# The last layer norm of a decoder layer: the last sums in two narrow parts, the root by ScalarE and one Newton step, shift vectors added by TensorE for three of four column quarters

## The chip, the cores and the metric

The kernel runs on one core of one Trainium2 chip. The core has TensorE (PE in the profile; its weight loads are PEld), VectorE (DVE), ScalarE (ACT), GpSimd (POOL) and SyncE (SP). SP and ACT also issue DMAs; the queues' own rows read SPq and ACTq. The metric is the device time of one execution in microseconds (us); before the change the median of three runs is 2263.68 us.

## The reference, cut to what matters

One decoder layer on 256 tokens of width 2048, all in float32. The change touches its last two lines alone:

```
alpha = (2.0 * DEPTH) ** 0.25
...
ple = jax.nn.sigmoid(h @ w_ple_gate[i]) * (p[i] @ w_ple_proj[i])
h = layer_norm(alpha * h + ple, ln_g[i, 3], ln_b[i, 3])

def layer_norm(x, g, b):
    mu = jnp.mean(xf, axis=-1, keepdims=True)
    var = jnp.mean(jnp.square(xf - mu), axis=-1, keepdims=True)
    y = (xf - mu) * lax.rsqrt(var + LN_EPS)
    return y * g + b
```

`h @ w_ple_gate` is a 256 x 2048 by 2048 x 2048 product. `p @ w_ple_proj` is made early in the kernel, parked in DRAM and read back as `ppr`. Each token's mean and variance go over all 2048 columns, so no value of a token can be normalised before the last column of that token is there.

## The kernel before, in words

Every large product is split for precision: the operands are cut into a high and a low part of the type fp32r, and a product is three matmuls (low x high, high x high, high x low; `Sum.add`, lines L394 to L396) of 128 x 128 weights and 512 moving columns, added up in PSUM. The weights from DRAM arrive as "units" of 256 rows by 1024 columns: SP issues the load into `rw_pg` (L169), ACT casts it to the high part `hw_pg` (L173), DVE subtracts to get the low part `lw_pg` (L177). Raw, high and low parts take one SBUF slot each out of 23, and a new tile takes a slot whose last use is over. A planner in the program sets the order in which these jobs stand among the others: it keeps count of the slots in use, `weights(n)` limits them to n, and `spend`, `after` and `clock` are its estimates of when DVE and TensorE get where. Its result is a fixed order on each engine. Each engine runs its instructions in that order and waits by semaphores.

The end of the kernel is `embedding`. The 256 tokens are two halves t = 0 and t = 1 of 128 tokens, one token to a partition; the columns are two blocks b = 0 and b = 1 of 1024. The sum before the norm, `y[b][:, t]`, reads `f2y` in the trace. A column block needs eight units, `w_pg` 0 to 7. For block 1 the first three units are used for both token halves as they come (`block`). The other five, HELD_END of them, are held and used for t = 0 first, then for t = 1, in column quarters c of 512. PSUM sums of block 0 read `w_pg` in the trace, those of block 1 `pg`.

`finish` (L1325 to L1334) takes a finished sum: ACT makes the sigmoid `sg` (L1327), DVE multiplies it by `ppr` (L1331), adds it to ALPHA times y (L1332) and takes the sums for mean and variance, bn_stats, per 512 columns (L1334). When all four quarters of a token half are in, `ln_stats` makes mean and variance of them (`mv`, bn_aggr, L528) and the reciprocal root by a start value from the bits and two steps (eight small DVE instructions, L491 to L516). `last_norm` then runs per quarter: `ln_normal`, that is (y - mean) * g (L536) and times root plus b (L537), and the store of 128 x 512 values (256 KB) to `out_h` (L1341). `g` and `b` are loaded to all partitions by `ln_vectors` (L522).

`later(n, job)` and `run_side` put a job n places on into the stream of units.

Of the kernel before, what the change touches and what calls it, by code (L numbers as in the profile page):

```python
# [8 lines left out]
F32 = mybir.dt.float32  # L9
# [21 lines left out]
SLOTS = 23  # L31
FRONT = 4
HELD = 3
HELD_END = 5
MATMUL = 0.227


# [76 lines left out]
def layer(ctx: ExitStack, tc: tile.TileContext, io):  # L114
# [208 lines left out]
    def done(u):  # L323
        room["used"] -= u.keeps
        fill()
# [16 lines left out]
    def later(n, job):  # L342
        while len(side) < n:
            side.append(idle)
        side.insert(n, job)
# [74 lines left out]
    def block(name, b, units, lhs, forms, sums, fold, before=None, host=False):  # L420
        sevens = [p for kind, p in units if kind == "S"]
        aux = None
        for j, (kind, p) in enumerate(units):
            if before is not None:
                before(j)
            u = take(name, b, p)
            if kind == "P":
                for c in range(2):
                    for kk in range(2):
                        some_products(u, p, lhs, sums, (0, 1), (c,), (kk,))  # L430
                    if host and not c:
# [86 lines left out]
    def ln_vectors(i):  # L518
        out = []
        for name in ("ln_g", "ln_b"):  # L520
            v = slot([P, D], F32, f"{name}{i}")
            sync.dma_start(v, io[name][0, i : i + 1, :].broadcast_to([P, D]))  # L522
            out.append(v)
        return out
# [8 lines left out]
    def ln_normal(y, t, mv, rstd, g, b, k0, nk):  # L533
        x = y[k0 // 8][:, t, k0 % 8 * P : (k0 % 8 + nk) * P]
        at = slice(k0 * P, (k0 + nk) * P)
        dve.scalar_tensor_tensor(x, x, mv[:, 0:1], g[:, at], ALU.subtract, ALU.mult)  # L536
        dve.scalar_tensor_tensor(x, x, rstd, b[:, at], ALU.mult, ALU.add)  # L537
# [96 lines left out]
    def put_by(b, pt):  # L634
# [77 lines left out]
    def plain(n):  # L712
        return [("P", p) for p in range(n)]
# [225 lines left out]
    def flat(ps):  # L939
        return ps.rearrange("p a n -> p (a n)")  # L940
# [375 lines left out]
        return norm  # L1316


    def embedding(ht, norm, y):
        weights(12)  # L1320
        stats = small.tile([P, 2, 4, 6], F32, tag="stats", name="plst", bufs=1)
        lhs = lambda k: (ht[:, k, :S], ht[:, k, S:])
        e = [load_columns(pp, b, "ppr") for b in range(2)]

        def finish(b, ps, sg, t, at):  # L1325
            sl, s = y[b][:, t, at], sg[:, t, at]
            act.activation(s, ps, AF.Sigmoid)  # L1327
            after(clock["pe"] + 0.8)
            n = at.stop - at.start
            spend(n, n, n)  # L1330
            dve.tensor_tensor(s, s, e[b][:, t, at], ALU.mult)  # L1331
            dve.scalar_tensor_tensor(sl, sl, ALPHA, s, ALU.mult, ALU.add)  # L1332
            for c in range(at.start // 512, at.stop // 512):
                dve.bn_stats(stats[:, t, 2 * b + c, :], y[b][:, t, c * 512 : c * 512 + 512])  # L1334

        def last_norm(t, mv, rstd):
            out = io["out"][0, t * P : (t + 1) * P]
            for c in range(4):
                ln_normal(y, t, mv, rstd, g, b, 4 * c, 4)
                at = slice(c * 512, c * 512 + 512)  # L1340
                (act if t and c % 2 else sync).dma_start(out[:, at], y[c // 2][:, t, c % 2 * 512 : c % 2 * 512 + 512])  # L1341
# [5 lines left out]
        finish(0, flat(ps[0]), sg, 0, whole)  # L1347
        later(0, lambda ps=ps, sg=sg: finish(0, flat(ps[1]), sg, 1, whole))
# [201 lines left out]
```

## Time and profile before

| | us |
|---|---|
| three runs, median (lowest to highest) | 2263.68 (2263.54 to 2264.49) |
| the profiled execution, its own time | 2265.43 |
| its span, first to last instruction | 2263.6 |
| TensorE busy in it | 2243.4 (99%) |
| DVE busy | 2018.6 (89%) |
| ACT busy | 1212.8 (54%) |
| granted TensorE clock, mean | 0.998 |

A row of a timeline reads: start, duration, engine, line of the kernel, operation, output <- inputs, size, count; a bracket at its end gives the time that the engine had stood idle and who ended it. A row of groups has the count, the busy time and the mean duration in ns. Matmuls overlap: each row lasts about 0.39 us, but the next starts 0.227 us later.

### The profile page before, as it was taken

The numbers are of one execution on the slowest core, as the hardware profiler recorded it, in microseconds if no ns is written. First come the engines' busy times: TensorE is split into PE (matmuls) and PEld (weight loads), VectorE is DVE, ScalarE is ACT, GpSimd is POOL, SyncE is SP. The second block draws the span as 40 slices with busy tenths as digits, with TensorE's granted clock in tenths as the row PEclk, the third lists the DMA queues.
The fourth block names the chain that finished last, engine by engine and source line by source line (L and its number), as shares of the span: only waits on it lengthen the run. The fifth ranks groups of instructions, "written<-read, shape, count | busy, mean of one in ns | idle before, by whom it ended". The sixth has DMA issues, their size and how long they took to land.

```text
span 2263.6 us, 26904 instructions
## 1 busy us (share of the span) xinstructions
PE 2243.4 (99%) x10379; PEld 1862.3 (82%) x10379; DVE 2018.6 (89%) x1773; ACT 1212.8 (54%) x1025; POOL 0.7 (0%) x6
## 2 busy tenths in 40 slices
PE   9999999999999999999999999999999999999997
PEld 7888888888888888888887888888888888888886
DVE  7999999999998788899899978989899999889876
ACT  6555555555554454655555545455555555555541
POOL 0000000000000000000000000000000000000000
PEclk9999999999999999999999999999999999999999
DMA  9665665655677545355566655776566566565761
GB/s 315 202 217 175 214 206 185 192 200 206 218 264 272 184 142 199 129 196 192 169 214 213 192 215 196 270 230 208 179 201 217 190 204 216 177 216 211 285 255 54
DMA packets 246560, 465.34 MB, mean 206 GB/s; under 512 B 17696, under 2 KB 125728, under 8 KB 243872
## 3 DMA queue, kind: packets, MB, share of 16 engines
q1 hardware_dynamic: 245040, 462.05, 60.5%
q8 instruction: 81, 1.33, 0.2%
q10 hardware_dynamic: 1392, 1.57, 0.2%
q14 instruction: 47, 0.39, 0.0%
HBM read 455.17 MB, written 8.39 MB: 205 GB/s over the span
## 4 chain that ended last, share of the span: by engine, by line
PE 96%; DVE 2%; DMA 1%; issue 1%; SPq 0%; ACT 0%; ACTq 0%; DVEq 0%
PE f1g L396 5%; PE f1g L395 5%; PE f1g L394 5%; PE f2g L396 4%; PE f2g L395 4%; PE f2g L394 4%; PE rqk L355 3%; PE aqk L355 2%; PE f2d L396 1%; PE f1d L396 1%; PE f2d L394 1%; PE f1d L395 1%; PE f1d L394 1%; PE f2d L395 1%; PE rqk L363 1%; PE f1e L396 1%
## 5 line engine op out<-in xcount | busy, mean ns | idle before, releaser
L177 DVE TENSOR_TENSOR lf_gu<-rf_gu,hf_gu 128x2048 fp32r<-128x2048 f32 x94 | 211.4, 2286 | 3.5 <-ACT hf_gu L173 3.5
L173 ACT CAST hf_gu<-rf_gu 128x2048 fp32r<-128x2048 f32 x94 | 177.3, 1908 | 27.9 <-DMA rf_gu<-in_f_gu 16.0
L241 DVE TENSOR_TENSOR luf_gu<-uf_gu,huf_gu 128x2048 fp32r<-128x2048 f32 x79 | 180.5, 2285 | 2.6 <-ACT huf_gu L233 2.5
L221 ACT CAST hbf_gu<-rf_gu 128x1536 fp32r<-128x1536 f32 x79 | 115.7, 1483 | 82.8 <-DMA rf_gu<-in_f_gu 67.5
L228 ACT CAST huf_gu<-uf_gu 128x1024 fp32r<-128x1024 f32 x79 | 83.1, 1052 | 133.1 <-DVE uf_gu L227 129.7
L394 PE MATMUL f1g<-hf_gu,xt 128*128 128x512 f32 x384 | 149.6, 390 | 1.5 <-ACT hf_gu L132 1.5
L396 PE MATMUL f1g<-lf_gu,xt 128*128 128x512 f32 x384 | 149.9, 390 | 0.3 <-DVE lf_gu L133 0.3
L395 PE MATMUL f1g<-hf_gu,xt 128*128 128x512 f32 x384 | 149.4, 389 | 0.0
L177 DVE TENSOR_TENSOR lf_down<-rf_down,hf_down 128x2048 fp32r<-128x2048 f32 x60 | 136.2, 2288 | 14.7 <-ACT hf_down L173 6.8
L173 ACT CAST hf_down<-rf_down 128x2048 fp32r<-128x2048 f32 x60 | 114.1, 1913 | 49.4 <-DMA rf_down<-in_f_down 15.1
L237 DVE TENSOR_TENSOR lbf_gu<-rf_gu,hbf_gu 128x1536 fp32r<-128x1536 f32 x79 | 138.3, 1751 | 0.0
L396 PE MATMUL f2g<-lf_gu,ht 128*128 128x512 f32 x328 | 127.6, 389 | 0.0
L394 PE MATMUL f2g<-hf_gu,ht 128*128 128x512 f32 x328 | 127.6, 389 | 0.0
L395 PE MATMUL f2g<-hf_gu,ht 128*128 128x512 f32 x328 | 127.6, 389 | 0.0
L233 ACT CAST huf_gu<-uf_gu 128x1024 fp32r<-128x1024 f32 x79 | 83.2, 1053 | 30.1 <-DVE uf_gu L232 30.1
L227 DVE TENSOR_TENSOR uf_gu<-rf_gu 128x1024 f32<-128x1024 f32 x79 | 96.3, 1219 | 0.0
L394 PEld LDWEIGHTS f1g<-hf_gu,xt 128*128 128x128 f32 x384 | 72.1, 188 | 17.2 <-ACT hf_gu L132 2.5
L396 PEld LDWEIGHTS f1g<-lf_gu,xt 128*128 128x128 f32 x384 | 72.1, 188 | 17.0 <-DVE lf_gu L133 2.0
L395 PEld LDWEIGHTS f1g<-hf_gu,xt 128*128 128x128 f32 x384 | 72.1, 188 | 14.9
L395 PEld LDWEIGHTS f2g<-hf_gu,ht 128*128 128x128 f32 x328 | 61.6, 188 | 12.8
L394 PEld LDWEIGHTS f2g<-hf_gu,ht 128*128 128x128 f32 x328 | 61.6, 188 | 12.8
L396 PEld LDWEIGHTS f2g<-lf_gu,ht 128*128 128x128 f32 x328 | 61.6, 188 | 12.8
(1307 smaller groups left out, 6369.9 us busy)
## 6 DMA issues: line engine op xcount, KB each, us to landing
rf_gu<-in_f_gu SPq DMA_DIRECT2D x192, 512.0 KB, 5.5
rf_down<-in_f_down SPq DMA_DIRECT2D x176, 512.0 KB, 4.5
rf_gu<-in_f_gu SPq DMA_DIRECT2D x317, 256.0 KB, 4.4
rw_rv<-in_w_rv SPq DMA_DIRECT2D x32, 512.0 KB, 4.6
rw_mix<-in_w_mix SPq DMA_DIRECT2D x32, 512.0 KB, 4.6
rw_pg<-in_w_pg SPq DMA_DIRECT2D x32, 512.0 KB, 4.7
rgr<-in_w_in_f SPq DMA_DIRECT2D x24, 512.0 KB, 4.6
rga<-in_w_in_f SPq DMA_DIRECT2D x20, 512.0 KB, 5.1
```

The costliest lines, as they stand in the source:

```text
L173: act.copy(self.hi, self.raw)
L177: dve.tensor_tensor(self.lo, self.raw, self.hi, ALU.subtract)
L221: act.copy(self.hb, self.raw[:, 1:])
L227: dve.tensor_tensor(u[:, 0:2], raw[:, 1:3], raw[:, 0:1].broadcast_to([P, 2, 512]), ALU.add)
L228: act.copy(hu[:, 0:2], u[:, 0:2])
L233: act.copy(hu[:, 2:], u[:, 2:])
L237: dve.tensor_tensor(lb, raw[:, 1:], hb, ALU.subtract)
L241: dve.tensor_tensor(lu, u, hu, ALU.subtract)
L355: pe.matmul(ps[:, f], u.tile_of(kk)[0][:, f * P : (f + 1) * P], rhs(k), start=k == 0, stop=k == KD - 1,)
L394: pe.matmul(o, al, bh, start=first, stop=False)
L395: pe.matmul(o, ah, bh, start=False, stop=False)
L396: pe.matmul(o, ah, bl, start=False, stop=self.left == 0)
```

## The change

- HELD_END goes from 5 to 6: two units of block 1 are used for both token halves at once, six are held. `weights(14)` is set before the block.
- For t = 1 the last 512 columns are summed in two parts of 256 columns. `Parts` splits the moving operand: a product is then six matmuls of 256 columns in place of three of 512.
- The order of the held work is written out: t = 0 first quarter, one unit of t = 1 first quarter, t = 0 second quarter, the rest of t = 1 first quarter, then the two narrow parts. `finish` follows each piece. Four quarters of t = 0 are normalised before the last pieces of t = 1 are finished.
- For t = 1 bn_stats goes by 256 columns, eight groups instead of four.
- The statistics, an intermediate matrix and six small vectors live in one new slot tile, `ends`.
- For t = 1, y is multiplied by -g ahead of the mean (`turned_sign`) in three of the four quarters.
- The root of t = 1: ACT takes sqrt(4 var + 4 eps), DVE its reciprocal `half`, and one Newton step gives `minus`, the negative reciprocal root. ACT runs one sqrt on a constant first (`four_eps`, set by POOL at the start), which brings the load of its function table with it.
- For three quarters of t = 1 TensorE makes b + (minus * mean) * g in PSUM: an identity times b, ahead of time, plus a diagonal matrix `across` (128 x 128, by DVE) times g. These are six matmuls in float32, not fp32r. DVE then needs one instruction for a quarter: (-g y) * minus + PSUM. The last quarter goes the old way, on DVE, and comes first.
- The store of the last quarter comes first, on ACT; the other three follow on SP, ACT, SP.

On DVE, around the last three units of weights (`lw_pg`) of block 1. The numbers in a unit's name are its place and a tile number, `ends` and `plst` hold the statistics. Before:

```order
L177 TENSOR_TENSOR lw_pg_4_16119<-rw_pg_4_16083,hw_pg_4_16117 128x2048
L1331 TENSOR_TENSOR sg_15990<-sg_15990,ppr_15834 128x1024
L1332 SCALAR_TENSOR_TENSOR f2y_14613<-f2y_14613,sg_15990 128x1024
L1334 BN_STATS plst<-f2y_14613 128x6 x2
L177 TENSOR_TENSOR lw_pg_5_16163<-rw_pg_5_16114,hw_pg_5_16161 128x2048
L1331 TENSOR_TENSOR sg_15990<-sg_15990,ppr_15834 128x1024
L1332 SCALAR_TENSOR_TENSOR f2y_14613<-f2y_14613,sg_15990 128x1024
L1334 BN_STATS plst<-f2y_14613 128x6 x2
L177 TENSOR_TENSOR lw_pg_6_16199<-rw_pg_6_16158,hw_pg_6_16197 128x2048
L177 TENSOR_TENSOR lw_pg_7_16227<-rw_pg_7_16194,hw_pg_7_16225 128x2048
```

After:

```order
L177 TENSOR_TENSOR lw_pg_4_16121<-rw_pg_4_16085,hw_pg_4_16119 128x2048
L1347 TENSOR_TENSOR sg_15992<-sg_15992,ppr_15835 128x1024
L1348 SCALAR_TENSOR_TENSOR f2y_14615<-f2y_14615,sg_15992 128x1024
L1351 BN_STATS ends<-f2y_14615 128x6 x2
L177 TENSOR_TENSOR lw_pg_5_16176<-rw_pg_5_16116,hw_pg_5_16172 128x2048
L177 TENSOR_TENSOR lw_pg_6_16178<-rw_pg_6_16136,hw_pg_6_16174 128x2048
L1347 TENSOR_TENSOR sg_15992<-sg_15992,ppr_15835 128x1024
L1348 SCALAR_TENSOR_TENSOR f2y_14615<-f2y_14615,sg_15992 128x1024
L1351 BN_STATS ends<-f2y_14615 128x6 x4
L177 TENSOR_TENSOR lw_pg_7_16219<-rw_pg_7_16169,hw_pg_7_16217 128x2048
L1376 SCALAR_TENSOR_TENSOR f2y_14615<-f2y_14615,ln_g_16128 128x1024
```

Unit 6 moved ahead of the second `finish` of block 0, unit 7 stands alone behind it, and the first sign turn follows. In the slots, the high part of unit 7 now takes the place of the high part of unit 1 of the same block, and the low part of unit 5 that of the high part of unit 0; before, these two waited for block 0's units and earlier loads alone. The slot of `ln_b` was that of a raw unit that DVE frees and is now that of a unit that TensorE frees; unit 6's load stands behind it on SP.

On ACT, the end of the program. Before:

```order
L1327 ACTIVATE sg_16133<-pg_16130 128x1024
L1327 ACTIVATE sg_16133<-pg_16131 128x512
L1327 ACTIVATE sg_16133<-pg_16132 128x512
L1341 DMA out_h<-f2y_14613 128x512
L1341 DMA out_h<-f2y_15427 128x512
```

After:

```order
L1343 ACTIVATE sg_16135<-pg_16132 128x512 x2
L1343 ACTIVATE sg_16135<-pg_16133 128x512
L1343 ACTIVATE sg_16135<-pg_16134 128x256
L1343 ACTIVATE sg_16135<-pg_16133 128x256
L1426 ACT_TABLE_LOAD
L1426 ACTIVATE ends<-four_eps 128x1
L1431 ACTIVATE ends<-mv_16461,four_eps 128x1
L1363 DMA out_h<-f2y_15429 128x512
L1363 DMA out_h<-f2y_14615 128x512
```

Three sigmoids became five smaller ones, and the table load with its two roots stands between the last sigmoid and the stores.

On DVE, the end of the program (`f2y_14613` and `f2y_14615` are columns 0 to 1023, `f2y_15427` and `f2y_15429` columns 1024 to 2047). Before:

```order
L516 SCALAR_TENSOR_TENSOR rstd_16394<-nb,ncur 128x1
L536 SCALAR_TENSOR_TENSOR f2y_14613<-f2y_14613,mv_16392,ln_g_16126 128x512
L537 SCALAR_TENSOR_TENSOR f2y_14613<-f2y_14613,rstd_16394,ln_b_16128 128x512
L536 SCALAR_TENSOR_TENSOR f2y_14613<-f2y_14613,mv_16392,ln_g_16126 128x512
L537 SCALAR_TENSOR_TENSOR f2y_14613<-f2y_14613,rstd_16394,ln_b_16128 128x512
L536 SCALAR_TENSOR_TENSOR f2y_15427<-f2y_15427,mv_16392,ln_g_16126 128x512
L537 SCALAR_TENSOR_TENSOR f2y_15427<-f2y_15427,rstd_16394,ln_b_16128 128x512
L536 SCALAR_TENSOR_TENSOR f2y_15427<-f2y_15427,mv_16392,ln_g_16126 128x512
L537 SCALAR_TENSOR_TENSOR f2y_15427<-f2y_15427,rstd_16394,ln_b_16128 128x512
```

After:

```order
L1355 BN_AGGR mv_16461<-ends 128x2
L1432 TENSOR_SCALAR ends<-mv_16461 128x1
L1433 RECIPROCAL ends<-ends 128x1
L1434 TENSOR_SCALAR ends<-ends 128x1
L1435 SCALAR_TENSOR_TENSOR ends<-ends 128x1
L1436 TENSOR_SCALAR ends<-ident,ends,mv_16461 128x128
L1437 TENSOR_SCALAR ends<-ends 128x1
L536 SCALAR_TENSOR_TENSOR f2y_15429<-f2y_15429,mv_16461,ln_g_16128 128x512
L537 SCALAR_TENSOR_TENSOR f2y_15429<-f2y_15429,ends,ln_b_16130 128x512
L1444 SCALAR_TENSOR_TENSOR f2y_14615<-f2y_14615,ends,pls_16455 128x512
L1444 SCALAR_TENSOR_TENSOR f2y_14615<-f2y_14615,ends,pls_16456 128x512
L1444 SCALAR_TENSOR_TENSOR f2y_15429<-f2y_15429,ends,pls_16457 128x512
```

Eight instructions of 512 columns became five, three of which read what TensorE left in PSUM (`pls`).

The diff:

```diff
-HELD_END = 5
+HELD_END = 6
...
+    four_eps = const.tile([P, 1], F32, name="four_eps")
+    nc.gpsimd.memset(four_eps, 4.0 * LN_EPS)
...
+    class Parts:
+        def __init__(self, parts):
+            self.parts = parts
+
+        def add(self, left, right):
+            for j, part in enumerate(self.parts):
+                part.add(left, tuple(x[:, 256 * j : 256 * j + 256] for x in right))
...
-        stats = small.tile([P, 2, 4, 6], F32, tag="stats", name="plst", bufs=1)
+        ends = slot([P, 256], F32, "ends")
+        stats = [ends[:, at : at + 6 * n].rearrange("p (a b) -> p a b", b=6) for at, n in ((128, 4), (152, 8))]
+        across = ends[:, :P]
+        root, v4, half, square, minus, plus = (ends[:, at : at + 1] for at in range(200, 206))
...
-            for c in range(at.start // 512, at.stop // 512):
-                dve.bn_stats(stats[:, t, 2 * b + c, :], y[b][:, t, c * 512 : c * 512 + 512])
-
-        def last_norm(t, mv, rstd):
...
+            size = (512, 256)[t]
+            for c in range(at.start, at.stop, size):
+                dve.bn_stats(stats[t][:, (1024 * b + c) // size, :], y[b][:, t, c : c + size])
...
+        def turned_sign(c, n):
+            x = y[c // 2][:, 1, c % 2 * 512 : c % 2 * 512 + n]
+            spend(n)
+            dve.scalar_tensor_tensor(x, x, -1.0, g[:, 512 * c : 512 * c + n], ALU.mult, ALU.mult)
+
         later(0, lambda ps=ps, sg=sg: finish(0, flat(ps[1]), sg, 1, whole))
-        g, b = ln_vectors(3)
+        later(1, lambda: turned_sign(0, 1024))
...
-        sums = sums_of([[ps[0][:, 0], ps[0][:, 1]], [ps[1][:, 0], ps[2][:, 0]]], plain(PAIRS))
+        sums = sums_of([[ps[0][:, 0], ps[0][:, 1]], [ps[1][:, 0], None]], plain(PAIRS))
+        parts = [Sum(v[:, :256], 2 * PAIRS) for v in (ps[2][:, 0], ps[1][:, 1])]
+        sums[1][1] = Parts(parts)
         n = PAIRS - HELD_END
+        weights(14)
         block("w_pg", 1, plain(n), lhs, None, sums, None)
+        run_side(len(side))
...
-        for t in range(2):
-            for c in range(2):
-                for u, p in zip(us, held):
-                    some_products(u, p, lhs, sums, (t,), (c,))
-                    if t and c:
-                        done(u)
-                if t:
-                    finish(1, sums[t][c].ap, sg, t, slice(512 * c, 512 * c + 512))
-            if not t:
-                finish(1, flat(ps[0]), sg, 0, whole)
-            last_norm(t, *ln_stats(stats[:, t], 3, t, LN_EPS))
+        more(0, 0)
+        finish(1, sums[0][0].ap, sg, 0, slice(0, 512))
+        more(1, 0, slice(0, 1))
+        more(0, 1)
+        finish(1, sums[0][1].ap, sg, 0, slice(512, 1024))
+        mv = moments(0)
+        rstd = small.tile([P, 1], F32, tag="rstd", name="rstd30")
+        rsqrt(rstd, mv[:, 1:2], 1, LN_EPS)
+        more(1, 0, slice(1, HELD_END))
+        for c in range(3):
+            normal(c)
+        finish(1, sums[1][0].ap, sg, 1, slice(0, 512))
+        turned_sign(2, 512)
+        normal(3)
+        for j, part in enumerate(parts):
+            for u, p in zip(us, held):
+                for kk in range(2):
+                    hi, lo = u.piece(1, kk)
+                    at = slice(256 * j, 256 * j + 256)
+                    part.add(half_of(lhs(2 * p + kk), 1), (hi[:, at], lo[:, at]))
...
+            finish(1, part.ap, sg, 1, slice(512 + 256 * j, 768 + 256 * j))
+        act.activation(root, four_eps, AF.Sqrt)
+        shifts = [banks("pls0")[:, j] for j in range(2)] + [banks("pls1")[:, 0]]
+        for c in range(3):
+            pe.matmul(shifts[c], ident, b[:, 512 * c : 512 * c + 512], start=True, stop=False)
+        mv = moments(1)
+        act.activation(root, mv[:, 1:2], AF.Sqrt, bias=four_eps, scale=4.0)
+        dve.tensor_scalar(v4, mv[:, 1:2], 4.0, 4.0 * LN_EPS, ALU.mult, ALU.add)
+        dve.reciprocal(half, root)
+        dve.tensor_scalar(square, half, half, v4, ALU.mult, ALU.mult)
+        dve.scalar_tensor_tensor(minus, square, 3.0, half, ALU.subtract, ALU.mult)
+        dve.tensor_scalar(across, ident, minus, mv[:, 0:1], ALU.mult, ALU.mult)
+        dve.tensor_scalar(plus, minus, -1.0, None, ALU.mult)
+        for c in range(3):
+            pe.matmul(shifts[c], across, g[:, 512 * c : 512 * c + 512], start=False, stop=True)
+        ln_normal(y, 1, mv, plus, g, b, 12, 4)
+        store(1, 3, act)
+        for c in range(3):
+            x = columns(y, c)
+            dve.scalar_tensor_tensor(x, x, minus, shifts[c], ALU.mult, ALU.add)
+            store(1, c, (sync, act, sync)[c])
```

`more(t, c)` adds the held units' products for one token half and quarter, `normal(c)` is `ln_normal` and store for t = 0, `moments(t)` is the bn_aggr, and `store` takes the queue as an argument. `ln_vectors(3)` is called one statement earlier than before.

More of the change, by code (lines that the diff above doesn't have):

```diff
@@ L1332, in finish, with moments, columns, store @@
             dve.scalar_tensor_tensor(sl, sl, ALPHA, s, ALU.mult, ALU.add)
-            for c in range(at.start // 512, at.stop // 512):
-                dve.bn_stats(stats[:, t, 2 * b + c, :], y[b][:, t, c * 512 : c * 512 + 512])
-        def last_norm(t, mv, rstd):
[L1337 to L1341, printed above, removed]
+            size = (512, 256)[t]
+            for c in range(at.start, at.stop, size):
+                dve.bn_stats(stats[t][:, (1024 * b + c) // size, :], y[b][:, t, c : c + size])
+        def moments(t):
+            mv = small.tile([P, 2], F32, tag="mv", name=f"mv3{t}")
+            dve.bn_aggr(mv, stats[t].rearrange("p a b -> p (a b)"))
+            return mv
+        def columns(v, c):
+            return v[c // 2][:, 1, c % 2 * 512 : c % 2 * 512 + 512]
+        def store(t, c, queue):
+            at = slice(c * 512, c * 512 + 512)
+            queue.dma_start(io["out"][0, t * P : (t + 1) * P, at], y[c // 2][:, t, c % 2 * 512 : c % 2 * 512 + 512])
         ps, sums = norm.front("w_pg", 0, lhs, plain(PAIRS))
@@ L1354, in embedding, with normal @@
+        parts = [Sum(v[:, :256], 2 * PAIRS) for v in (ps[2][:, 0], ps[1][:, 1])]
+        sums[1][1] = Parts(parts)
         n = PAIRS - HELD_END
+        weights(14)
         block("w_pg", 1, plain(n), lhs, None, sums, None)
+        run_side(len(side))
         held = range(n, PAIRS)
         us = [take("w_pg", 1, p) for p in held]
-        for t in range(2):
-            for c in range(2):
-                for u, p in zip(us, held):
-                    some_products(u, p, lhs, sums, (t,), (c,))
-                    if t and c:
-                        done(u)
-                if t:
-                    finish(1, sums[t][c].ap, sg, t, slice(512 * c, 512 * c + 512))
-            if not t:
-                finish(1, flat(ps[0]), sg, 0, whole)
-            last_norm(t, *ln_stats(stats[:, t], 3, t, LN_EPS))
+        def normal(c):
+            ln_normal(y, 0, mv, rstd, g, b, 4 * c, 4)
+            store(0, c, sync)
@@ new lines, in more @@
+        def more(t, c, at=slice(0, HELD_END)):
+            for u, p in list(zip(us, held))[at]:
+                some_products(u, p, lhs, sums, (t,), (c,))
+        more(0, 0)
[7 more added lines that the diff above has]
+        more(1, 0, slice(1, HELD_END))
@@ new lines, in embedding @@
+        for c in range(3):
[9 more added lines that the diff above has]
+                    part.add(half_of(lhs(2 * p + kk), 1), (hi[:, at], lo[:, at]))
+                if j:
+                    done(u)
+            finish(1, part.ap, sg, 1, slice(512 + 256 * j, 768 + 256 * j))
```

1 line of the change is left out of this document (added).

## The prediction

> **What bounds the kernel now.** I read the page first: busy shares, then the chain that ended last.
>
> ```profile
> span 2263.6 us, 26904 instructions
> PE 2243.4 (99%) x10379; PEld 1862.3 (82%) x10379; DVE 2018.6 (89%) x1773; ACT 1212.8 (54%) x1025; POOL 0.7 (0%) x6
> PE 96%; DVE 2%; DMA 1%; issue 1%; SPq 0%; ACT 0%; ACTq 0%; DVEq 0%
> ```
>
> TensorE is busy for 99% of the span and is 96% of the chain. Nothing is gained before its last product, so the change must pay behind it. The timelines of the three engines from the start of column block 1 show that tail:
>
> ```profile
> 2205.51 0.39 PE L394 MATMUL pg<-hw_pg,ht 128*128 128x512 f32 x1
> 2248.81 0.39 PE L396 MATMUL pg<-lw_pg,ht 128*128 128x512 f32 x1
> ...
> 2235.63 1.03 ACT L1327 ACTIVATE sg<-pg 128x1024 f32<-128x1024 f32 x1 [22.56 <-PE pg L396]
> 2242.43 0.60 ACT L1327 ACTIVATE sg<-pg 128x512 f32<-128x512 f32 x1 [5.77 <-PE pg L396]
> 2249.23 0.60 ACT L1327 ACTIVATE sg<-pg 128x512 f32<-128x512 f32 x1 [6.20 <-PE pg L396]
> ...
> 2240.54 0.26 DVE L528 BATCH_NORM_AGGREGATE mv<-plst 128x2 f32<-128x24 f32 x1
> 2242.50 0.75 DVE L536 SCALAR_TENSOR_TENSOR f2y<-f2y,mv,ln_g 128x512 f32<-128x512 f32 x1
> 2248.30 0.68 DVE L1331 TENSOR_TENSOR sg<-sg,ppr 128x512 f32<-128x512 f32 x1
> 2250.35 0.68 DVE L1331 TENSOR_TENSOR sg<-sg,ppr 128x512 f32<-128x512 f32 x1
> 2252.51 0.26 DVE L528 BATCH_NORM_AGGREGATE mv<-plst 128x2 f32<-128x24 f32 x1
> 2254.46 0.75 DVE L536 SCALAR_TENSOR_TENSOR f2y<-f2y,mv,ln_g 128x512 f32<-128x512 f32 x1
> 2259.59 0.75 DVE L537 SCALAR_TENSOR_TENSOR f2y<-f2y,rstd,ln_b 128x512 f32<-128x512 f32 x1
> ```
>
> The block's 192 products start 43.30/191 = 0.2267 us apart; the last ends at 2249.20. The span ends 14.4 us later: 11.14 us of DVE (to 2260.34) and 3.26 us for the last store and the end of the program. DVE has no wait in these 11.14 us and comes late into them: at 2248.30 it begins on a quarter of t = 1 whose products were done before 2242.43, because the four normalisations of t = 0 (2242.50 to 2248.30, 1.45 a quarter) stand ahead. A quarter's `finish` takes 2.16 (2250.35 to 2252.51, so 0.72 a step), moments and root 1.95 (2252.51 to 2254.46), four quarters 5.88.
>
> **The change, part by part.** *Narrow products on TensorE.* 48 matmuls of 512 columns become 96 of 256. The nearest row is a group of such matmuls with 128 x 128 weights elsewhere; the next two rows are for the float32 products below:
>
> ```profile
> L363 PE MATMUL aqk<-ht,lf_(20, 0)_5329 x16: 277/283/283, 755.5 to 757.3; 128*128 128x256 f32 x16
> 1082.95 0.59 PE L1062 MATMUL rs<-rq,rk 128*128 128x256 f32 x2
> 1083.38 0.38 PE L1063 MATMUL rs<-rq,rk 128*128 128x128 f32 x2
> ```
>
> Sixteen in 1.8 us from first to last start: 0.12 each. So 96 x 0.12 - 48 x 0.2267 = +0.64 us. Bounds: 0.113 (half a wide one) makes it 0, 0.13 makes it +1.6. I take 0.12. The stream then ends at 2205.51 + 144 x 0.2267 + 96 x 0.12 = 2249.67; the last matmul, in flight 0.28, is out at 2249.83.
>
> *Weights, from the order.* Two units now take 11.04 us (each 18 wide, 12 narrow), so held work starts at 2216.55, and unit 7 is wanted five units of 6 x 0.2267 later, at 2223.35, its low part at 2223.8 (before: 2227.3 and 2227.7).
>
> ```profile
> 2196.73 0.33 SPq L522 DMA_DIRECT2D ln_b<-in_ln_b  x1
> 2200.04 6.24 SPq L169 DMA_DIRECT2D rw_pg<-in_w_pg  x4
> 2205.96 1.90 ACT L173 CAST hw_pg<-rw_pg 128x2048 fp32r<-128x2048 f32 x1
> 2206.09 1.23 DVE L1331 TENSOR_TENSOR sg<-sg,ppr 128x1024 f32<-128x1024 f32 x1 [7.20 <-ACT sg L1327]
> 2215.73 4.47 DVE L177 TENSOR_TENSOR lw_pg<-rw_pg,hw_pg 128x2048 fp32r<-128x2048 f32 x2
> ...
> 2210.00:2215.00 5.00, 5.00 (x23) 4.14 (x23) 4.93 (x4) 2.49 (x2) 0.00 (x0) 1.00 0.00 0
> ```
>
> Before, the last low part was ready at 2220.2. Now `ln_b` waits for TensorE's freeing of a slot, where unit 6's load waited (2200.04), and that load and unit 7's stand behind it on SP; ACT casts unit 6 at about 2208 and unit 7 only when TensorE has left unit 1, 2216.6 to 2218.5. On DVE unit 5 waits for TensorE to leave unit 0 (2211.2), then unit 6 to 2215.7, a `finish` of 1024 columns with four narrow bn_stats, 3.9 (twice 1.25, four times 0.36), then unit 7, 2219.6 to 2221.9. That is 1.9 us ahead of need: no stall. Cost nothing, but the cover has shrunk from 7.5 us to 1.9; beyond it each us late costs one.
>
> *DVE up to the last part.* t = 0 second quarter is out at 2234.4 (2216.55 + 36, 6 and 36 products), its sigmoid at 2235.03. From 2235.06 DVE has 2.16 + 1.95 + three normalisations 4.35 + `finish` of t = 1 first quarter 2.2 + sign turn 0.70 + fourth normalisation 1.45 + first narrow part 1.35 = 14.2, to 2249.2. The second narrow part's sigmoid is out at 2249.83 + 0.03 + 0.38 = 2250.24 (0.38 on the line through 1.03 and 0.60). DVE waits 1.0 us for it: what had made it late is gone, and TensorE and ACT are late next. The first sign turn (1.2 us) fits before 2225, where DVE waits for TensorE. POOL's memset of 128 x 1 joins six instructions that take 0.7 us in all, at the start, beside the first loads: nothing, at most 0.1.
>
> *Last part and mean.*
>
> ```profile
> L465 DVE TENSOR_TENSOR sums<-f2a 128x256 f32<-128x256 f32 x4 | 1.7, 422 | 0.0
> L1107 DVE SCALAR_TENSOR_TENSOR ret<-ro,gmv,eve 128x256 f32<-128x256 f32 x16 | 6.6, 476 | 0.0
> L1091 DVE BATCH_NORM_STATS2 gst<-ro 128x6 f32<-128x256 f32 x16 | 6.5, 407 | 3.6 <-PE ro L1086 3.6
> L1092 DVE BATCH_NORM_AGGREGATE gmv<-gst 128x2 f32<-128x6 f32 x16 | 2.9, 182 | 0.6
> L503 DVE TENSOR_SCALAR nb<-ncur,nv 128x1 f32<-128x1 f32 x8 | 2.2, 273 | 0.3
> L1011 DVE RECIPROCAL asm<-asm 128x4 f32<-128x4 f32 x8 | 1.4, 178 | 0.3
> L1015 DVE TENSOR_SCALAR asc<-asc,asm 128x128 f32<-128x128 f32 x16 | 3.9, 284 | 0.3
> ```
>
> Three steps of 0.42, 0.45 and 0.41 with gaps: 1.35, to 2251.6. bn_aggr took 0.18 on 6 numbers and 0.26 on 24, so 0.37 on 48: variance at 2252.0.
>
> *Root.* The table load has to be over by then. Rows of two earlier loads:
>
> ```profile
> 2.77 1.28 ACT L1420 ACT_TABLE_LOAD   x1 [2.77 <-issue]
> 4.06 0.20 ACT L1420 ACTIVATE warm<-warm 128x1 f32<-128x1 f32 x1
> 797.00 0.58 ACT L883 COPY ra<-aqk 128x512 f32<-128x512 f32 x1 [6.92 <-PE aqk L355]
> 797.61 1.28 ACT L995 ACT_TABLE_LOAD   x1
> ```
>
> The load starts 0.03 after the work ahead of it and the next instruction 0.01 behind it: 2250.27 to 2251.55, constant root to 2251.75. Hidden under 1.7 us of DVE, by 0.25. Then root 0.2 to 0.3 with the hop to ACT, reciprocal 0.2, square 0.3, `minus` 0.2, `across` 0.34 (the 0.28 above has one vector operand, not two): 2253.35. From bn_aggr's end to the first normalising step that is 1.4, against 1.69 before; the root itself saves little.
>
> *Normalising.* DVE: last quarter from 2253.4, 0.78 + 0.67, then three steps 0.67 apart, the third at 2256.18. TensorE: a float32 product of 256 columns took 0.43 (1082.95 to 1083.38, two records), so 0.86 for 512; three of them and 0.17 in flight from 2253.4 end at 2256.15. Both sides meet, so a cheaper product would give nothing. The b products run in TensorE's idle time, 2249.7 to 2252.3. Last DVE step 0.72: 2256.9.
>
> *Stores.*
>
> ```profile
> L1341 ACTq DMA_DIRECT2D out_h<-f2y x2: 351/356/362, 2257.5 to 2260.4; - x2
> DMA to landing us min/median/max: 2.2/2.3/2.3
> ```
>
> They come 0.7 apart, not 1.45. Bounds 0 and +0.7; I take +0.1, since two queues share them.
>
> *Sum.* The tail behind TensorE's last product was 11.14 + 3.26 = 14.4 and will be 7.07 + 3.36 = 10.43; TensorE ends 0.63 later: -3.3 us, span 2260.3. The profiled execution took 2265.43, 1.8 more than its span, and stands 1.75 above the median of the runs; the difference is carried to the median: 2263.68 - 3.3 = 2260.4, 0.15% faster. A measurement of this kernel can tell about 0.2% (4.5 us) from no change, so this counts as within.
>
> **Rivals.** *TensorE waits for unit 7* (slower). The place and the 1.9 us are above. Lost gain from 5.2 us late, slower by 0.2% from 9.7 us. For it: three loads of 1 MB now leave SP within about a us of 2200, and two casts wait for TensorE itself. Against: issued at 2200 to 2206 they had landed by 2210 (the window from 2210 to 2215 moved nothing, its last figure), and unit 7's cast waits until 2216.6 anyway. Time 2268 and more; 9%, of it 8% beyond 0.2%.
>
> [...]
>
> *TensorE's clock has halved when `across` comes.* The windows behind the last product:
>
> ```profile
> 2253.00:2254.00 1.00, 0.00 (x0) 0.00 (x0) 0.85 (x5) 0.00 (x0) 0.00 (x0) 1.00 0.00 0
> 2254.00:2255.00 1.00, 0.00 (x0) 0.00 (x0) 0.93 (x4) 0.00 (x0) 0.00 (x0) 0.62 0.00 0
> ```
>
> The granted clock (third from the end) fell about 5.0 us after TensorE stopped. Here it stands idle for 1.1 us between b and `across`. At half speed three products would take 2.6 us more: 2263.0; 4%. [...]
>
> *All small terms at their low ends* (faster by over 0.2%): narrow products at 0.113 (-0.6), DVE's narrow steps, bn_aggr and `across` 0.3 less, the hop to ACT 0.1, stores 0.1, and 0.4 from elsewhere in the run: 2258.9; 17%. Against: TensorE's 0.12 is measured.
>
> **Chances.** Forecast 65%, small terms low 17%, stall 9%, drain 5%, clock 4%. Faster 0.17; same 0.65 + 0.05 + 0.04 + 0.01 = 0.75; slower 0.08. The range reaches from the low ends, 2258.9, past the half clock, to 2263.2, and leaves out the stall and part of the low case.
>
> **What would show it.** Right: last narrow product ends near 2249.8, without a gap of TensorE at unit 7; DVE idles about 1 us before the second narrow part; the constant root ends before bn_aggr; the three last DVE steps run nearly without waits; the last one ends near 2256.9. Wrong: TensorE idle near 2223; the root waiting behind the table load; DVE waiting for `pls` by more than 0.3 a step; a last store landing more than 2.6 us after its issue.

## The result, and the profile after

The changed kernel takes 2261.85 us, the median of 22 runs (2259.84 to 2264.34); the kernel before, run beside it, 2264.85 us (22 runs, 2263.50 to 2267.64). The ratio is 0.9987 with a 95% interval from 0.9981 to 0.9993: 3.0 us between the medians, 0.13%, faster. The interval lies below 1, and the gain is smaller than the 0.2% that the prediction set as its bound. The kernel before itself came out 1.17 us higher than in the three runs that the prediction started from (2263.68).

Two profiles cannot simply be subtracted. The profiled execution after took 2264.34 us, the longest of the 22 runs, with a span of 2262.6, only 1.0 us less than before, although its tail is 2.8 us shorter. So I measure from S, the start of the first product of column block 1. In the changed kernel's timeline of TensorE that is 2207.35; before it was 2205.51.

```profile
2207.13 0.39 PE L396 MATMUL w_pg<-lw_pg,ht 128*128 128x512 f32 x1
2207.35 0.39 PE L394 MATMUL pg<-hw_pg,ht 128*128 128x512 f32 x1
```

| from S, us | before | predicted | after |
|---|---|---|---|
| TensorE's last `pg` product ends | 43.69 | 44.32 | 44.37 |
| variance of t = 1 ready | 47.26 | 46.49 | 46.57 |
| `across` ready | - | 47.84 | 48.12 |
| TensorE's third `across` product ends | - | 50.64 | 51.02 |
| DVE's last instruction ends | 54.83 | 51.39 | 51.80 |
| span ends | 58.09 | 54.79 | 55.25 |

The tail is 2.84 us shorter, which agrees with the runs' 3.0. The first lines of the page after:

```profile
span 2262.6 us, 27044 instructions
PE 2251.5 (100%) x10439; PEld 1870.4 (83%) x10439; DVE 2019.0 (89%) x1778; ACT 1215.7 (54%) x1030; POOL 0.7 (0%) x7
```

DVE's timeline, from the low part of unit 7 to the last step:

```profile
2221.26 2.27 DVE L177 TENSOR_TENSOR lw_pg<-rw_pg,hw_pg 128x2048 fp32r<-128x2048 f32 x1
...
2250.64 0.43 DVE L1351 BATCH_NORM_STATS2 ends<-f2y 128x6 f32<-128x256 f32 x1
2252.17 0.42 DVE L1347 TENSOR_TENSOR sg<-sg,ppr 128x256 f32<-128x256 f32 x1 [1.10 <-ACT sg L1343]
...
2253.55 0.37 DVE L1355 BATCH_NORM_AGGREGATE mv<-ends 128x2 f32<-128x48 f32 x1
...
2254.35 0.16 DVE L1433 RECIPROCAL ends<-ends 128x1 f32<-128x1 f32 x1 [0.23 <-ACT ends L1431]
...
2255.12 0.35 DVE L1436 TENSOR_SCALAR ends<-ident,ends,mv 128x128 f32<-128x128 f32 x1
...
2256.89 2.26 DVE L1444 SCALAR_TENSOR_TENSOR f2y<-f2y,ends,pls 128x512 f32<-128x512 f32 x3
```

TensorE's timeline behind its last `pg` product:

```profile
2251.56 2.74 PE L1429 MATMUL pls<-ln_b,ident 128*128 128x512 f32 x6
2255.53 2.84 PE L1439 MATMUL pls<-ln_g,ends 128*128 128x512 f32 x6 [1.23 <-DVE ends L1436]
```

ACT's timeline from the last sigmoid to the root:

```profile
2251.76 0.38 ACT L1343 ACTIVATE sg<-pg 128x256 f32<-128x256 f32 x1 [3.94 <-PE pg L396]
2252.16 1.28 ACT L1426 ACT_TABLE_LOAD   x1
2253.45 0.20 ACT L1426 ACTIVATE ends<-four_eps 128x1 f32<-128x1 f32 x1
2254.02 0.29 ACT L1431 ACTIVATE ends<-mv,four_eps 128x1 f32<-128x1 f32 x1 [0.36 <-DVE mv L1355]
```

DVE's first bracket is the new wait of 1.10 us for the second narrow part: DVE is no longer late, TensorE and ACT are. The constant root ends at 2253.65, 0.27 us before the variance (2253.92), so the table load is hidden. TensorE waits 1.23 us for `across`, and its three products are done at 2258.37. The chain of work that ended last passes over these products, where before it was DVE alone:

```profile
2255.12 0.36 DVE ends L1436
2255.48 0.04 issue
2255.53 2.86 PE pls L1439 x6
2258.38 0.02 issue
2258.41 0.75 DVE f2y L1444
```

### The profile page after: what moved, and what is told of

The parts are those of the page before. It is cut to its first block, busy times and chain, and to the rows that moved or that the text cites. A ratio compares the mean times of both kernels' runs of the same rounds, so it can differ in the third digit from the quotient of the medians.

```text
span 2262.6 us, 27044 instructions
## 1 busy us (share of the span) xinstructions
PE 2251.5 (100%) x10439; PEld 1870.4 (83%) x10439; DVE 2019.0 (89%) x1778; ACT 1215.7 (54%) x1030; POOL 0.7 (0%) x7
## 4 chain that ended last, share of the span: by engine, by line
PE 98%; DVE 0%; DMA 0%; issue 0%; ACT 0%; SPq 0%; ACTq 0%; DVEq 0%
PE f1g L394 5%; PE f1g L396 5%; PE f1g L395 5%; PE f2g L395 4%; PE f2g L396 4%; PE f2g L394 4%; PE rqk L355 3%; PE aqk L355 2%; PE f2d L396 1%; PE f1d L396 1%; PE f1d L394 1%; PE f2d L394 1%; PE f2d L395 1%; PE f1d L395 1%; PE rqk L363 1%; PE f2e L396 1%
```

## The experiments

DVE's end is read from S in each profile. In the one repetition it agreed within 0.01 us, while the time of the changed kernel's 22 runs spreads over 4.5 us. All figures of the table are in us, the first and the last two from S.

| run | `across` ready | TensorE's `across` products | DVE ends | span ends |
|---|---|---|---|---|
| before | - | - | 54.83 | 58.09 |
| after | 48.12 | 2.84 | 51.80 | 55.25 |
| after_again | 48.12 | 2.84 | 51.80 | 55.22 |
| order_only | - | - | 54.36 | 57.63 |
| all_on_dve | - | - | 53.64 | 57.02 |
| dve_root | 48.98 | 4.54 | 54.37 | 57.68 |
| wide_last | 48.51 | 4.54 | 53.89 | 57.24 |
| wide_warm | 48.51 | 2.84 | 52.19 | 55.53 |
| late_b | 48.12 | six products | 56.99 | 60.35 |
| no_constant_root | 49.40 | 4.43 | 54.66 | 58.03 |
| late_unit | 51.17 | 2.84 | 54.85 | 58.23 |
| three_engines | 48.12 | 0.96 (fp32r) | 50.94 | 55.16 |
| three_engines_384 | 50.00 | 0.97 (fp32r) | 52.82 | 57.04 |

### The order of work alone (order_only)

```diff
-        for j, part in enumerate(parts):
...
-            finish(1, part.ap, sg, 1, slice(512 + 256 * j, 768 + 256 * j))
-        act.activation(root, four_eps, AF.Sqrt)
...
+        for u, p in zip(us, held):
+            some_products(u, p, lhs, sums, (1,), (1,))
+            done(u)
+        finish(1, sums[1][1].ap, sg, 1, slice(512, 1024))
+        rsqrt(rstd, mv[:, 1:2], 1, LN_EPS)
+        for c in range(4):
+            ln_normal(y, 1, mv, rstd, g, b, 4 * c, 4)
+            store(1, c, (sync, act)[c % 2])
```

> Keeps the changed order of the held work (HELD_END 6, weights(14), t = 1 begun early, four normalisations of t = 0 ahead of the last pieces) and takes back all the rest: one last part of 512 columns, DVE's eight-step root, no sign turns, all four quarters of t = 1 on DVE. Measured from S, the first product of block 1, to DVE's last end: before 54.83 us, after 51.80. Theory (the order alone only takes DVE's lateness out of the front of the tail; the three quarters handed to TensorE carry most of the gain): last wide sigmoid out at S + 44.3, finish 2.16, moments and root 1.95, four quarters 5.88, so S + 54.3 to 54.5, 0.4 us better than before. Rival (DVE's lateness was the brake and the order carries the gain): near S + 52. In the device time the theory gives -0.4 us (0.02%), the rival -2.8 us (0.12%).

DVE ended at S + 54.36, as the theory said; the ratio to before is 0.9997 (0.9987 to 1.0006). Taking the lateness out of DVE's queue gave 0.47 us. In this run's timeline DVE even waits 2.89 us for the last sigmoid:

```profile
2251.32 0.69 DVE L1347 TENSOR_TENSOR sg<-sg,ppr 128x512 f32<-128x512 f32 x1 [2.89 <-ACT sg L1343]
2252.05 0.69 DVE L1348 SCALAR_TENSOR_TENSOR f2y<-f2y,sg 128x512 f32<-128x512 f32 x1
```

So the lateness that I read from the profile before had been a symptom: with it gone, the last sigmoid sets the same chain of finish, root and four quarters 0.47 us earlier, and no more.

### Three quarters handed back to DVE (all_on_dve)

```diff
-        for c in range(3):
-            pe.matmul(shifts[c], ident, b[:, 512 * c : 512 * c + 512], start=True, stop=False)
...
-        ln_normal(y, 1, mv, plus, g, b, 12, 4)
-        store(1, 3, act)
-        for c in range(3):
-            x = columns(y, c)
-            dve.scalar_tensor_tensor(x, x, minus, shifts[c], ALU.mult, ALU.add)
+        for c in range(4):
+            ln_normal(y, 1, mv, plus, g, b, 4 * c, 4)
...
```

> The changed kernel with TensorE's shift vectors and the sign turns taken out: all four quarters of t = 1 normalised on DVE, two steps each; ScalarE's root and the two narrow parts stay. Theory: DVE's stretch from the root on is four quarters of 1.45 us behind an end of the root at about S + 47.8, so its last end at S + 53.65, 1.85 us later than in the changed kernel (51.80). Rival (DVE waits for TensorE's float32 products by 1.2 us in the changed kernel, so handing the work back costs next to nothing): S + 51.8 to 52.2.

S + 53.64 against 53.65 expected: handing three quarters to TensorE is worth 1.84 us. The sum of the parts follows from the two runs: order 0.47 (54.83 to 54.36), narrow parts and ScalarE's root together 0.72 (to 53.64), TensorE's products 1.84 (to 51.80); together 3.03. These are the worths in this order of steps: no run has the later steps without the new order of work, so what they would bring with DVE late is not shown.

### DVE's root in the changed kernel (dve_root)

```diff
-        act.activation(root, four_eps, AF.Sqrt)
...
-        act.activation(root, mv[:, 1:2], AF.Sqrt, bias=four_eps, scale=4.0)
...
-        dve.scalar_tensor_tensor(minus, square, 3.0, half, ALU.subtract, ALU.mult)
+        rsqrt(plus, mv[:, 1:2], 1, LN_EPS)
+        dve.tensor_scalar(minus, plus, -1.0, None, ALU.mult)
```

> The changed kernel with DVE's eight-step reciprocal root for t = 1 in place of ScalarE's root and the Newton step, and one more small instruction for the sign; no table load at the end. Theory (a small DVE instruction costs 0.2 to 0.25 us with its gap; ScalarE's way saves what five of them cost, less two hops): `across` 0.65 us later, DVE's last end at S + 52.45. Rival (two hops between the engines eat it, the table load delays it): S + 51.8 or earlier.

DVE ended at S + 54.37, 2.57 us later than after: four times my 0.65. `across` was 0.86 late, in the theory's direction. The other 1.7 us are in the products, in this run's timeline of TensorE:

```profile
2254.06 4.54 PE L1434 MATMUL pls<-ln_g,ends 128*128 128x512 f32 x6 [2.10 <-DVE ends L1432]
```

DVE's timeline shows the steps that waited for them:

```profile
2257.11 0.75 DVE L1439 SCALAR_TENSOR_TENSOR f2y<-f2y,ends,pls 128x512 f32<-128x512 f32 x1 [0.96 <-PE pls L1434]
2258.64 0.75 DVE L1439 SCALAR_TENSOR_TENSOR f2y<-f2y,ends,pls 128x512 f32<-128x512 f32 x1 [0.78 <-PE pls L1434]
```

The same six matmul records took 4.54 us instead of 2.84, and DVE waited twice. The windows of the same run give the reason; the granted clock is the third figure from the end:

```profile
2254.02:2254.52 0.50, 0.46 (x1) 0.30 (x2) 0.50 (x1) 0.00 (x0) 0.00 (x0) 1.00 0.00 0
2254.52:2255.02 0.50, 0.50 (x2) 0.19 (x1) 0.47 (x2) 0.00 (x0) 0.00 (x0) 0.86 0.00 0
2255.02:2255.52 0.50, 0.50 (x2) 0.34 (x1) 0.50 (x2) 0.00 (x0) 0.00 (x0) 0.50 0.00 0
...
2258.02:2258.52 0.50, 0.50 (x1) 0.00 (x0) 0.00 (x0) 0.00 (x0) 0.00 (x0) 0.73 0.00 0
```

TensorE's clock fell to half in the midst of the products, after 2.10 us of idleness, and came back 3.4 us later.

### One wide last part (wide_last)

```diff
-        for j, part in enumerate(parts):
-            for u, p in zip(us, held):
...
-            finish(1, part.ap, sg, 1, slice(512 + 256 * j, 768 + 256 * j))
+        for u, p in zip(us, held):
+            some_products(u, p, lhs, sums, (1,), (1,))
+            done(u)
+        finish(1, sums[1][1].ap, sg, 1, slice(512, 1024))
```

> The changed kernel with one last part of 512 columns for t = 1 in place of two of 256; bn_stats stays at 256 columns. Theory: TensorE ends 0.64 us earlier (S + 43.7), but the sigmoid takes 0.60 instead of 0.38 and DVE's three steps on 512 columns 2.2 instead of 1.37, so the variance and with it DVE's last end comes 0.4 us later, S + 52.2. Rival (the second narrow part costs TensorE 0.64 us and brings nothing, since DVE is late anyway): 0.2 us or more earlier, S + 51.6.

`across` came 0.39 later, as expected, but DVE ended 2.09 later, at S + 53.89. TensorE was done 0.69 us earlier and `across` came later, so it stood idle for 2.31 us, and the products took 4.54 us once more. Both expectations had missed this.

### The wide part, with TensorE kept busy (wide_warm)

```diff
+        spare = banks("pls2")[:, 0]
+        for c in range(2):
+            pe.matmul(spare, ident, b[:, 512 * c : 512 * c + 512], start=True, stop=True)
```

> The wide last part of the run above it, with two more float32 products of identity and b into a PSUM tile that nobody reads, behind the three b products: TensorE then stands idle for about 0.6 us instead of 2.3 before `across` comes. Nothing of the computation is left out. With the wide part alone the three `across` products took 4.54 us (2.84 in the changed kernel) and DVE's last end came at S + 53.89. Theory (the 2.3 us of idleness let the granted clock fall to 0.50, and that was the whole difference): clock 1.00 throughout, three products 2.84 again, DVE's last end at S + 52.2, which is the 0.4 us later than the changed kernel that the wide part itself costs. Rival (TensorE is slowed by DVE's and ACT's traffic at that moment, or by the wide part's place): products stay above 4 us, S + 53.9.

Two products that nobody reads bring DVE's end 1.70 us forward against the kernel without them. TensorE's timeline without them (wide_last):

```profile
2248.38 2.73 PE L1422 MATMUL pls<-ln_b,ident 128*128 128x512 f32 x6
2253.42 4.54 PE L1432 MATMUL pls<-ln_g,ends 128*128 128x512 f32 x6 [2.31 <-DVE ends L1429]
```

And with them (wide_warm):

```profile
2248.89 2.74 PE L1422 MATMUL pls<-ln_b,ident 128*128 128x512 f32 x6
2251.47 1.88 PE L1425 MATMUL pls<-ln_b,ident 128*128 128x512 f32 x4
2253.93 2.84 PE L1435 MATMUL pls<-ln_g,ends 128*128 128x512 f32 x6 [0.59 <-DVE ends L1432]
```

The granted clock stayed at 1.00 until 2260, past DVE's end, and the end came at S + 52.19. So the wide part itself costs 0.39 us, and the fall of the clock 1.70. In the changed kernel the gap is 1.23 us, and the clock stayed at 1.00 through all its products.

### The b products on the path (late_b)

```diff
-        for c in range(3):
-            pe.matmul(shifts[c], ident, b[:, 512 * c : 512 * c + 512], start=True, stop=False)
...
-            pe.matmul(shifts[c], across, g[:, 512 * c : 512 * c + 512], start=False, stop=True)
+            pe.matmul(shifts[c], across, g[:, 512 * c : 512 * c + 512], start=True, stop=False)
+            pe.matmul(shifts[c], ident, b[:, 512 * c : 512 * c + 512], start=False, stop=True)
```

> The changed kernel with the three identity times b products moved from TensorE's idle time to behind each `across` times g product. TensorE then is idle for 3.8 us before `across` and has six products behind it instead of three. If the price is only the three products, 3 x 0.86: DVE's last end at S + 54.4 (after: 51.80). If the clock falls as it did with the wide part (the products then take 1.7 us each for some 4 us): S + 56.2. If DVE were the bound and TensorE beside it: S + 52.5 or less. I expect S + 56.2.

S + 56.99, still 0.8 beyond the half-clock estimate. The clock had already fallen 1.6 us before the first product and came back only 5.2 us behind it, so more products ran slowly than I had reckoned. The b products thus do two things in TensorE's idle time: reckoned at 0.86 us a product they keep 2.6 us off the path, and they keep the clock up, which is the other 2.6 of the 5.19 us between this run and the changed kernel.

### No early root on a constant (no_constant_root)

```diff
-        act.activation(root, four_eps, AF.Sqrt)
```

> The changed kernel without the constant root ahead of time: the table load then stands with the root itself, which waits for DVE's variance. Theory (the early root hides the load of 1.28 us): the root comes 1.25 us later, `across` ends at S + 49.4; TensorE is idle for 2.5 us before it, so the clock falls as with the wide part and the products take 4.5 us: DVE's last end near S + 54.7. If the clock holds: S + 53.05. Rival (the load is done ahead of the wait anyway, so the early root brings nothing): S + 51.8.

S + 54.66, as expected. ACT's timeline in this run has the load behind the wait for the variance:

```profile
2251.82 1.28 ACT L1430 ACT_TABLE_LOAD   x1 [1.86 <-DVE mv L1355]
2253.11 0.29 ACT L1430 ACTIVATE ends<-mv,four_eps 128x1 f32<-128x1 f32 x1
```

`across` is 1.28 late, the length of the load and nothing beside it. The rest, 1.58 us, is the clock again: TensorE had been idle for 2.50 us. In this execution one line of code is worth 2.86 us, nearly the whole gain.

### Unit 7 late (late_unit)

```diff
-            act.copy(self.hi, self.raw)
+            for _ in range(4 if self.key == ("w_pg", 1, 7) else 1):
+                act.copy(self.hi, self.raw)
```

> The changed kernel with ScalarE's cast of unit 7's high part made four times over, so it is out some 5.7 us later. In the changed kernel the cast ends near S + 13.1 and the low part at S + 16.2, and TensorE wants the high part at S + 17.8 and the low part at S + 18.3. Theory (2.1 us of cover, behind it each us late costs one): low part near S + 21.9, TensorE stands for about 3 to 3.6 us in the held work, and everything from its last product on keeps its distance: DVE's last end at S + 54.8 to 55.4. Rival (the later order or DVE's own waits absorb it): S + 51.8 to 53.

TensorE's timeline shows the two waits, for the high and for the low part:

```profile
2224.10 0.50 PE L395 MATMUL pg<-hw_pg,ht 128*128 128x512 f32 x1 [0.88 <-ACT hw_pg L174]
2226.43 0.50 PE L397 MATMUL pg<-lw_pg,ht 128*128 128x512 f32 x1 [1.59 <-DVE lw_pg L178]
```

The low part was ready at S + 21.20, 5.0 us later than after (2223.53, S + 16.18). TensorE's last `pg` product ended 3.04 us later and DVE's last instruction 3.05 later, at S + 54.85. So the cover is 2.0 us if behind it each us late costs one; this one run fits that, and its 5 us late cancel the gain.

### A cheaper product, and less for DVE (three_engines)

```diff
+        across = slot([P, P], F32R, "across")
...
+        gr = slot([P, D], F32R, "gr")
...
+            act.copy(gr[:, :1536], g[:, :1536])
...
+        act.mul(diag, ident, minus)
-            pe.matmul(shifts[c], across, g[:, 512 * c : 512 * c + 512], start=False, stop=True)
+            pe.matmul(shifts[c], across, gr[:, 512 * c : 512 * c + 512], start=False, stop=c < 2)
+        pe.matmul(shifts[2], diag, columns(y, 2), start=False, stop=True)
...
+        act.copy(columns(y, 2), shifts[2])
+        store(1, 2, act)
```

> The changed kernel with its last bound, TensorE's three float32 `across` products (0.86 us each), made cheaper, and with less work for DVE: `across` and a copy of g are rounded to fp32r (ScalarE makes the copy earlier, in its idle time), so a product of 512 columns takes 0.23 us; quarter 2 is made by TensorE wholly (a third, float32 product adds diag(minus) times x) and brought out of PSUM by ScalarE. DVE then has the last quarter (1.45 us) and two steps of 0.67 instead of three. Nothing is left out; the mean's term is rounded. Theory (behind `across` TensorE's products are the bound, DVE's three steps stand 0.3 us under them): DVE's last end at S + 51.0 to 51.2 (after: 51.80), ScalarE's eviction out by S + 50.6, so 0.6 to 0.8 us off the tail; device time 0.15 to 0.2% below the kernel before. Rival (DVE is the bound and the stores, which now come closer together, take it back): S + 51.0 for DVE but the span's end at S + 55.1 or later (after: 55.25).

DVE ended at S + 50.94, 0.86 us earlier, as the theory said. The span ended at S + 55.16, 0.09 earlier, as the rival said. Device time: 2261.47 us, ratio to before 0.9987 (0.9978 to 0.9996), not distinguishable from the change. The windows of this run, whose last two figures are the DMA engines' busy share and GB/s, show who took the gain:

```profile
2254.50:2255.50 1.00, 0.00 (x0) 0.00 (x0) 0.48 (x1) 0.19 (x1) 0.00 (x0) 1.00 0.92 346
2255.50:2256.50 1.00, 0.00 (x0) 0.00 (x0) 0.00 (x0) 0.00 (x0) 0.00 (x0) 1.00 1.03 385
2256.50:2257.50 1.00, 0.00 (x0) 0.00 (x0) 0.00 (x0) 0.00 (x0) 0.00 (x0) 1.00 0.92 318
```

The four last stores are 1 MB, issued within 1.3 us, and they take 2.8 us at about 380 GB/s. DVE is done at 2254.98, while the DMA engines work till about 2257.4. From the first of these stores on, the transfers are the bound: ACT issues it at S + 49.66 in this kernel (2253.70) and at S + 49.66 in the changed kernel (2257.01), so the spans end 0.09 apart.

### The same, cut into 384 and 128 (three_engines_384)

```diff
+CUTS = (0, 384, 512)
...
-                    at = slice(256 * j, 256 * j + 256)
+                    at = slice(CUTS[j], CUTS[j + 1])
```

> The run above it, with the last 512 columns cut into 384 and 128 instead of 256 and 256. Nothing is left out. No row here shows fp32r products of 384 or 128 columns. If their spacing falls with the columns (0.17 and 0.06 us): TensorE ends at S + 43.7, the sigmoid takes 0.3, DVE's three steps on 128 columns about 0.8, and DVE's last end comes at S + 50.1 to 50.4. If 128 columns take the 0.12 us that 256 columns take (the weights' load of 0.19 us a product is what sets it): TensorE ends 1.6 us later than in the run above (48 more products of 0.12 in the place of 48 of 0.06, and the 384's 0.17), at about S + 46.5, and DVE's last end comes at S + 51.8 or later. I lean to the first.

The second case came: TensorE's `pg` products ended at S + 46.68, 2.3 us later than in the run above (the expectation's 1.6 does not fit its own S + 46.5), and DVE at S + 52.82. Two neighbouring rows of TensorE's timeline for each width give the spacing:

```profile
2246.06 0.33 PE L396 MATMUL pg<-hw_pg,ht 128*128 128x384 f32 x1
2246.24 0.33 PE L397 MATMUL pg<-lw_pg,ht 128*128 128x384 f32 x1
...
2250.15 0.28 PE L396 MATMUL pg<-hw_pg,ht 128*128 128x128 f32 x1
2250.26 0.28 PE L397 MATMUL pg<-lw_pg,ht 128*128 128x128 f32 x1
```

A product of 128 columns comes every 0.11 us, hardly less than the 0.12 of 256, so this cut does not pay. Other unequal cuts were not tried.

### The changed kernel again (after_again)

> The changed kernel once more, unchanged, for the place of S in another execution. Theory (the 1.84 us by which S lay later in the changed kernel's first profile than in the profile of before is a spread from execution to execution): S somewhere between 2203.6 and 2207.4, where the nine other profiles have it, and the tail behind it the same within 0.05 us (DVE's last end S + 51.80). Rival (the change delays the program upstream, through the order of loads): S at 2207.3 again.

S was 2203.88 and DVE's end S + 51.80. In all profiles S lies between 2203.68 and 2207.35, whatever the tail. The two executions of the changed kernel part in the stretch of `ga` products: the product ahead of them starts at 1238.05 in the first and 1238.42 in the second, the last of them at 1325.49 and 1321.98. It is the same program, so this is a spread from execution to execution, and S after says nothing on the change. The traces show what the first lost there. Its TensorE waited twice for DVE, 1.14 and 1.18 us, where the second waited once, 0.34 us:

```profile
1239.57 0.50 PE L394 MATMUL ga<-hga,ht 128*128 128x512 f32 x1 [1.14 <-DVE eve L483]
1241.71 0.61 PE L394 MATMUL ga<-hga,ht 128*128 128x512 f32 x1 [1.18 <-DVE eve L485]
```

Behind these waits its granted clock was at half for 3.41 us, where the second kept 1.00; the products then started 0.43 us apart in place of 0.23, some 1.6 us in all:

```profile
1241.89:1245.30 3.41, 3.41 (x9) 2.63 (x9) 3.38 (x3) 0.00 (x0) 0.00 (x0) 0.50 0.43 157
```

Of the other profiles only that of order_only has such a fall there, from 1241.51 to 1244.92, and these two have the latest S, 2207.35 and 2206.97.

## Why the prediction was right

- **What bounds the kernel.** Right: TensorE to its last product, then the tail. The reading of the tail was half right: DVE's lateness was no cause but a cover, as the order alone showed (0.47 us).
- **Narrow products on TensorE.** Right: +0.64 predicted; the last product ended 0.68 later from S. wide_last gave the same 0.69 the other way.
- **Weights.** Right: 1.9 us of slack said, 2.0 to 2.1 found. The forecast that 5.2 us late would cost the whole gain came out at 5.0.
- **DVE up to the last part; last part and mean.** Right: wait of 1.0 said, 1.10 found; variance 0.08 later than said.
- **Root.** Mis-sized by 0.2: 1.35 from variance to `across` said, 1.55 measured. The root starts 0.10 behind the variance, takes 0.29, and the reciprocal starts 0.04 behind it; `across` takes 0.35. The remark that the root saves little was wrong in what follows from it: without ScalarE's root, `across` came 0.86 later in dve_root, and the clock fell.
- **Normalising.** Mechanism right, the two sides did nearly meet: TensorE's products ended 2.90 behind `across` (2.80 said), and DVE's third step waited 0.2 us for the last. The claim that a cheaper product would give nothing was not tried by itself. On DVE it could win no more than this 0.2 us; three_engines, which takes work off DVE as well, shows that the stores would have kept most of it.
- **Stores.** +0.1 said, +0.19 measured (3.45 from DVE's end to the span's end, 3.26 before). Here the four stores are one transfer already: the DMA engines are busy at 0.97 to 1.01 in the windows from 2258 to 2260.
- **Sum.** -3.3 said, -2.84 measured in the tail. The 0.46 between them are 0.08 up to the variance, 0.20 of Root, 0.13 of Normalising and some 0.05 of Stores. The forecast of 2260.4 lies 1.45 below the median; 1.17 of that is the start (2263.68 where more runs gave 2264.85), the other 0.3 the sum. That the start lay low is chance, and no merit or fault of the working.
- **The rivals.** Unit 7: no wait; its price was right. The drain that has 5% among the chances, a pause of ACT around the table load: no run shows it. The sigmoid ends at 2252.14, the load starts at 2252.16, the constant root follows 0.01 behind its end, and in no_constant_root the load put 1.28 us on the path and no more. The half clock: it did not come here (1.00 through all products), but I had dismissed it with the wrong number, the 5.0 us after TensorE's stop that the profile before showed. One us more of idleness was enough in three experiments, and the fall then cost 1.6 to 1.7 us, not the 2.6 reckoned. So the outcome was right, and the reason given for it was not.

## What to carry to other kernels

Time each part of a tail from an event that the change cannot reach; two executions of one program that part by 3.5 us before that event hide a gain of 3. Where a matrix product follows a serial stretch, look at the idle gap ahead of it: behind 2.31 us of it in wide_last, three products took 4.54 us in place of 2.84. Useful early products, or failing those two that nobody reads, kept the clock up here, and the two were worth 1.7 us in wide_warm. And when the last engine gets faster, look at once at what drains its output: here 1 MB of stores ended an improvement of 0.86 us at 0.09.

## What the runs showed of the hardware

In the windows of 0.5 us around the tails the granted clock reads 1.00, 0.50 or, in single windows, a value between them. Such a value, taken as the mean over the two sides of one change, tells its moment: with 0.86 in 2254.52 to 2255.02, dve_root's clock fell at 2254.88, and with 0.73 in 2258.02 to 2258.52 it was back at 2258.29, 3.41 us later. The same working gives 3.41 us in wide_last and in no_constant_root, and 6.82, twice as much, in late_b.

```profile
2253.36:2253.86 0.50, 0.44 (x1) 0.39 (x2) 0.50 (x3) 0.00 (x0) 0.00 (x0) 0.72 0.00 0
...
2256.86:2257.36 0.50, 0.50 (x2) 0.25 (x1) 0.23 (x1) 0.00 (x0) 0.00 (x0) 0.87 0.61 238
```

These are wide_last's two windows: 2253.58 and 2256.99. How long TensorE had stood idle does not by itself tell when the clock fell. From its last product to the fall it was 5.0 us before, 5.1 in all_on_dve, 4.9 in three_engines, 4.6 in order_only, 4.1 in the profile after and 3.3 in wide_warm, but 2.3 us in late_b, from its last `pg` product. With gaps of 2.10, 2.31 and 2.50 us ahead of the `across` products the clock fell 0.8, 0.2 and 1.1 us behind their start (dve_root, wide_last, no_constant_root). With the changed kernel's 1.23 us it held through the products in both profiles. But among the `ga` products it fell at 1241.89 in the profile after, behind gaps of 1.14 and 1.18 us, and at 1241.51 in order_only, behind 0.42 and 1.18:

```profile
1238.09:1241.51 3.42, 1.82 (x7) 0.91 (x7) 2.85 (x4) 3.06 (x3) 0.00 (x0) 1.00 1.03 358
1241.51:1244.92 3.41, 3.41 (x9) 2.63 (x9) 3.38 (x3) 0.00 (x0) 0.00 (x0) 0.50 0.68 242
```

Before, the gaps there were 0.25 and 1.17 us, and the clock stayed at 1.00. What the clock goes by is therefore open, and the 5.0 us that the prediction used are the reading of one profile. How often the clock falls in the three kernels with gaps of 2.1 to 2.5 us was not tried: each has one profile.
